# Expert weights in pairs of buffers, eight neighbouring rows per partition, in a diffusion backbone layer with expert-choice experts

## The chip, the cores and the metric

The kernel runs on one NeuronCore of a Trainium2 chip. The metric is the time of one execution on the device in microseconds (us). TensorE is called PE (PEld for its weight loads), VectorE DVE, ScalarE ACT, GpSimd POOL and SyncE SP. PEq, ACTq and SPq are the instruction queues of these engines.

## The reference

One layer works on 512 latent tokens of 1,024 features (and on 256 context tokens, which only feed the recurrence). First comes a token mixer: RMSNorm with adaLN shift and scale, one input projection, a Fourier branch and a recurrent branch, a gated merge, an output projection, a gated residual. Then the part that this change touches:

```
h  = rmsnorm(x) * (1 + sc2) + sh2                 # 512 x 1024
scores = softmax(h @ w_router)                    # 16 experts
g, idx = top 64 tokens of each expert by score
xg  = h[idx]                                      # 64 x 1024 for each expert
hid = silu(xg @ w_gate[e]) * (xg @ w_up[e])       # w_gate, w_up: 1024 x 1536
out = (hid @ w_down[e]) * g                       # w_down: 1536 x 1024
x  += g2 * scatter_add(out, idx)
y   = rmsnorm(x) * final_g
```

All of it is float32. The three weight matrices of 16 experts are 302 MB, read once from HBM.

## The kernel before

The first 405 us or so are the token mixer. Its weights come through staging tiles in pieces 256 columns (1 KB) wide. After it, w_out is applied in four column quarters, each token tile is squared and turned for the router, the softmax over the 16 experts is taken, and tokens are ranked by score.

Expert weights come in **units** of 128 x 1,536 floats, 6 KB on each partition (786,432 bytes). An expert has 24: eight of w_gate, eight of w_up, eight of w_down. Unit q of w_gate holds rows 128q to 128q+127, one row per partition, so partition p of unit k meets feature 128k+p. Units of w_down put six neighbouring rows on a partition and cut that run of 24 KB in four. The list `units` has them in the order in which PE reads them. The last expert's w_down is cut into nine pieces by output columns, with final_g ahead of them.

`eload()` issues the load of the next unit on SP's queue. Buffers go round: `NR = (14, 5, 1)` says how many lie in each of three rings (which open one after the other as the memory of the mixer and of the router comes free), two more are `held` in the staging tiles `wd` and `we`, and units 14 and 15 use two tiles lent by the staging area. So 22 units can be in SBUF. Each ring buffer is loaded again when PE has read it. 24 loads are issued ahead of the first expert; after that each unit read by `up_gate` (L1161) or by w_down's loop (L1260) is followed by one `eload()`. SP works through its loads strictly in order, and a load waits there for its buffer and for its turn among the semaphores that count DMAs. 

For two experts at a time, tokens are gathered by matmul: `gather_k` (L1133) multiplies a 128 x 128 block of x (the stationary operand, features 128k to 128k+127 of 128 tokens) with a one-hot matrix `oh` of the chosen tokens, over four token tiles. Each float32 matmul of this kind is two instructions. `gather_out_k` (L1139, L1141) applies shift (`modc`) and scale (`s2`), which lie feature 128k+p on partition p, column k, and writes `xg`. The gather of a pair comes at the end of the odd expert before it; experts 0 and 1 are gathered piece by piece (`one_k`, tile `xa`) within the first experts.

Within an expert: gate units, with the scatter of the previous expert between them (L1180); silu on ACT (L1222); up units, with the ranking of the expert after next; the gather in odd experts; six transposes of the hidden values, `sl[:, j:FH:6]`, every sixth element (L1248); w_down's units; the scaled output. At expert 2 ACT's queue copies half of `g2` into the spare end of `we` (L1240).

The end of the kernel adds the last expert's output in three column parts, normalises and stores four tiles `o` that reuse ring buffers (L1275 to L1305).

The shift's contribution to the router is made at L992 (matmuls `pb`) and L993 (copy to `bias`); behind it `ada_red` (L293, L300) reduces the last adaLN part, and L995 scales the router's weights. L430 is the matmul of w_out, L949 transposes x for the router.

Of the kernel before, what the change touches and what calls it, by code (L numbers as in the profile page):

```python
# [21 lines left out]
NT = T // P  # L22
# [12 lines left out]
def tables():  # L35
    quarter = D // 4
    f32 = np.float32
    freqs = np.exp(f32(-np.log(10000.0)) * np.arange(quarter, dtype=f32) / f32(quarter)).astype(f32)
    emb = np.zeros((64, 2, 512), f32)
    for i, n in ((0, T // GRID_W), (1, GRID_W)):  # L40
        ang = np.arange(n, dtype=f32)[:, None] * freqs
        emb[:n, i] = np.concatenate([np.sin(ang), np.cos(ang)], axis=-1)
    d = np.arange(P)
    a = 2 * np.pi * ((d[:, None] * d) % P) / P
    t = np.arange(258)
    dft_c = np.zeros((P, 387), f32)
    dft_c[:, 0:65] = np.cos(a[:, 0:65])
    dft_c[:, 65:129] = np.sin(a[:, 0:64])
    dft_c[0, 129:386] = np.where(np.arange(257) % 2, -1.0, 1.0) / 256.0
    dft_t = np.zeros((P, 2, 2, 258), f32)  # L50
    for b in range(2):
        m = ((P * b + d[:, None]) * t) % T
        dft_t[:, 0, b] = np.where(t < 257, np.cos(2 * np.pi * m / T) / 256.0, 0.0)
        dft_t[:, 1, b] = np.where((t < 256) & (m % 256 != 0), -np.sin(2 * np.pi * m / T) / 256.0, 0.0)
    p = np.arange(P)
    cst = np.zeros((P, 211), f32)
    cst[:, 0:128] = np.eye(P)
    for v in range(2):
        cst[:, 128 + v] = (p % 32 == v)
    for e in range(NE):  # L60
        cst[:, 130 + e] = (p % 32 == e)
    cst[:, 146:210] = np.arange(64)
    cst[:, 210] = p % 64
    tri = (p[:, None] < p[None, :]).astype(f32)
    sel = np.zeros((8, NT, P), f32)
    for n in range(NT):
        sel[:, n] = np.arange(8)[:, None] == 2 * n + p // 64
    rs = np.concatenate([emb[:8, 0], sel.reshape(8, -1)], axis=1)
    return {"rs": rs, "ce": np.concatenate([emb[:, 1]] * 2), "dft_c": dft_c, "dft_t": dft_t, "cst": cst, "tri": tri}


V_N2, V_CW, V_CB, V_LAM, V_BA, V_BI = 8, 16, 48, 56, 72, 88
# [4 lines left out]
def layer(ctx: ExitStack, tc: tile.TileContext, I, out):  # L77
    nc = tc.nc
    pe, act, dve, pool = nc.tensor, nc.scalar, nc.vector, nc.gpsimd
# [10 lines left out]
    def flat(ap, off, dims):  # L90
        return bass.AP(tensor=ap.tensor, offset=ap.offset + off, ap=[list(d) for d in dims])
# [6 lines left out]
    stage, close_stage = sb("stage")  # L98
# [9 lines left out]
    def gt(name):  # L108
        return ps.tile([P, 2, 512], F32, tag="g", bufs=2, name=name)
# [4 lines left out]
    x = keep.tile([P, NT, D], F32, name="x")  # L114
# [9 lines left out]
    s2 = keep.tile([P, KD], F32, name="s2")  # L124
# [739 lines left out]
    close_gp()  # L864
    close_hl()

    NR = (14, 5, 1)
    rings = [None] * 3
    edge, close_edge = open_pool("edge", side="right")
    edge.tile([P, 120], F32, name="edge")  # L870
# [10 lines left out]
    def eload():  # L881
        n = ring["n"]
        if n >= len(units):
            return
        ring["n"] += 1
        e, wn, q = units[n]
        if 0 <= n - NR[0] < 2:
            t = stage.tile([P, 2048], F32, tag="raw", bufs=AHEAD, name=f"lent{n}")[:, 0:DE]
        else:
            m, i = (n if n < NR[0] else n - 2) % (sum(NR) + 2), 0  # L890
            while i < 3 and m >= NR[i]:
                m, i = m - NR[i], i + 1
            t = rings[i].tile([P, DE], F32, tag="ew", bufs=NR[i], name=f"ew{n}") if i < 3 else held[m]
        if e == NE:
            t = t[:, 0:D]
            nc.sync.dma_start(t, flat(I["final_g"], 0, [[0, P], [1, D]]))
            EW["fg"] = t
            return
        src = I[wn][0, e]
        if wn == "w_down_e":  # L900
            if e == NE - 1:
                c0, cw, k0, nk = q
                f, j = divmod(k0, 6)
                t = t[:, 0:cw * nk].rearrange("p (k d) -> p k d", k=nk)
                nc.sync.dma_start(t, src[FH * f:FH * f + FH, c0:c0 + cw].rearrange("(p k) d -> p k d", k=6)[:, j:j + nk])
            else:
                f, j = divmod(q, 4)
                nc.sync.dma_start(t, src[FH * f:FH * f + FH, :].rearrange("(p k) d -> p (k d)", k=6)[:, DE * j:DE * j + DE])
        else:
            nc.sync.dma_start(t, src[P * q:P * q + P, :])  # L910
        EW[e, wn, q] = t


    rt, close_rt = sb("rt", "right")
    bias = rt.tile([P, NE], F32, name="bias")
    lg = rt.tile([P, NT, NE], F32, name="lg")
    mx = rt.tile([P, 2, NT], F32, name="mx")
    xT = rt.tile([P, KD, P], F32, name="xT")
# [79 lines left out]
    wa = stage.tile([P, 4, 512], F32, tag="raw", bufs=AHEAD, name="wa")  # L998
    sB, oh, trit = wa[:, 0, :], wa[:, 1, :].rearrange("p (n c) -> p n c", n=NT), wa[:, 2, 0:P]
    nc.sync.dma_start(trit, I["tri"])  # L1000
    eload()
    eload()
    dve.memset(oh, 0.0)

# [61 lines left out]
    eload()  # L1066
    g20 = we[:, DE:2048]
    sl = wc[:, 1280:2048]
# [61 lines left out]

    def gather_k(a, k, q):
        for n in range(NT):
            pe.matmul(a[k // 4][:, P * (k % 4) + q.start:P * (k % 4) + q.stop], x[:, n, P * k:P * k + P],  # L1133
                      oh[:, n, q], start=n == 0, stop=n == NT - 1)

    def gather_out_k(a, k, q):
        src = a[k // 4][:, P * (k % 4) + q.start:P * (k % 4) + q.stop]
        if k % 2 or k < 3 and q == h0:
            act.activation(xg[:, k, q], src, AF.Identity, bias=modc[:, 24 + k, 0:1], scale=s2[:, k:k + 1])  # L1139
        else:  # L1140
            dve.tensor_scalar(xg[:, k, q], src, s2[:, k:k + 1], modc[:, 24 + k, 0:1], op0=OP.mult, op1=OP.add)  # L1141

    def gather():
        a = [at("xg0"), at("xg1")]
# [8 lines left out]
    def up_gate(e, wn, name, hooks):  # L1153
        t = mps.tile([P, 2, 512], F32, tag=name, bufs=1, name=name)
        c = CAP * (e % 2)
        for k in range(KD):
            w = EW.pop((e, wn, k))
            for n in range(2):
                for f in range(2):
                    o = FH * f + 384 * n  # L1160
                    pe.matmul(t[64 * f:64 * f + 64, n, 0:384], xg[:, k, c:c + CAP], w[:, o:o + 384],  # L1161
                              start=k == 0, stop=k == KD - 1, tile_position=(0, 64 * f))
            if (e, wn) != (0, "w_up_e") or k < KD - 2:
                eload()
            for f in hooks.get(k, ()):
                f()
        return t
# [42 lines left out]
    for e in range(NE):  # L1210
# [44 lines left out]
        for q in range(KD):  # L1255
            w = EW.pop((e, "w_down_e", q))
            f = q // 4
            for i in range(3):
                j, dh = divmod(3 * (q % 4) + i, 2)
                pe.matmul(yp[64 * dh:64 * dh + 64, :], hT[j // 3][:, j % 3, 64 * f:64 * f + 64], w[:, 512 * i:512 * i + 512],  # L1260
                          start=f == 0 and j == 0, stop=f == 1 and j == 5, tile_position=(0, 64 * dh))
            eload()
# [9 lines left out]
    ov = out[0].rearrange("(n p) d -> p n d", p=P)  # L1272
    act.activation(ssb[:, 7:8], eps_t, AF.Sqrt)
    e = NE - 1
    os = [rings[0].tile([P, D], F32, tag="ew", bufs=NR[0], name=f"o{n}") for n in range(NT)]  # L1275
    sst = (ss[:, 0:NT], ssb[:, 0:NT], ss[:, 4:4 + NT])

    def out_a(p, n, mid=None):
# [111 lines left out]
```

## Time and profile before

| | us |
|---|---|
| median of three runs | 1171.66 |
| lowest, highest | 1169.88, 1172.23 |
| the profiled execution | 1173.57 |
| its span, first to last instruction | 1171.7 |

| engine | busy us | share of the span |
|---|---|---|
| PE | 1134.9 | 97% |
| PEld | 678.5 | 58% |
| DVE | 548.8 | 47% |
| ACT | 293.4 | 25% |
| POOL | 115.3 | 10% |

The profiled execution is one run of its own, a little longer than its span, since the launch and the end lie around the span. Busy shares are averages over the mixer and the experts, which have different limits. Matmuls overlap in PE's pipeline, so a PE that is busy all the time is not a PE at its peak. TensorE's granted clock is 0.996 of its full 2.4 GHz over the span. HBM reads are 364.43 MB, 313 GB/s over the span.

### The profile page before, as it was taken

Reading aid. Unit: us, or ns where it says so; the run is one execution under the profiler, and the core shown is the slowest. Engines: PE = TensorE matmul, PEld = TensorE weight load, DVE = VectorE, ACT = ScalarE, POOL = GpSimd, SP = SyncE. Lnnn points to the kernel's source line nnn. Section 1 sums busy time; section 2 is a strip of 40 time slices with the busy share of each in tenths; the row PEclk is TensorE's granted clock in tenths of the full one; section 3 lists DMA queues with packets and bytes.
Section 4 is the critical chain, followed back from the end, with each engine's and each line's share of the span. In section 5 each row is a group of like instructions: output and inputs, shape, how many; then the busy total and the mean of one; then the engine's idle time right before and its main releaser. Section 6 shows DMA issues by size and latency. Waiting matters only on the chain. (4 is left out here: it accounts for less than half of the span.)

```text
span 1171.7 us, 16760 instructions
## 1 busy us (share of the span) xinstructions
PE 1134.9 (97%) x6888; PEld 678.5 (58%) x6888; DVE 548.8 (47%) x1090; ACT 293.4 (25%) x457; POOL 115.3 (10%) x120
## 2 busy tenths in 40 slices
PE   8999999999999999999999999999999999999986
PEld 4778777777888996545445445454454344444333
DVE  4455989877776854332333342342332332332124
ACT  5462776665322132101001001001001001001004
POOL 5173343421000000000000000000000000000002
PEclk9999999999999999999999999999999999999998
DMA  8924322233546597899999999999999999999995
GB/s 309 298 74 128 126 81 72 100 108 108 180 158 202 187 415 295 308 369 420 369 425 423 424 424 424 424 423 424 424 423 424 424 424 423 423 425 423 424 414 214
DMA packets 115435, 368.01 MB, mean 314 GB/s; under 512 B 8912, under 2 KB 61656, under 8 KB 115232
## 3 DMA queue, kind: packets, MB, share of 16 engines
q1 hardware_dynamic: 112688, 363.52, 78.4%
q0 software_dynamic: 1088, 2.18, 0.6%
q10 hardware_dynamic: 1584, 1.25, 0.4%
q8 instruction: 54, 0.88, 0.3%
q14 instruction: 21, 0.17, 0.0%
HBM read 364.43 MB, written 2.10 MB: 313 GB/s over the span
## 5 line engine op out<-in xcount | busy, mean ns | idle before, releaser
L1161 PE MATMUL G<-ew,g 128*64 128x384 f32 x960 | 171.5, 493 | 2.5 <-DMA ew<-in_w_gate_e 2.0
L1161 PE MATMUL U<-ew,g 128*64 128x384 f32 x928 | 166.3, 493 | 6.8 <-DMA ew<-in_w_up_e 6.7
L1186 DVE TENSOR_TENSOR ac<-ac,sc 128x512 f32<-128x512 f32 x112 | 71.9, 684 | 97.5 <-PE sc L1180 97.5
L1161 PEld LDWEIGHTS G<-ew,g 128*64 128x64 f32 x960 | 63.0, 136 | 85.1 <-issue 64.3
L1161 PEld LDWEIGHTS U<-ew,g 128*64 128x64 f32 x928 | 60.6, 136 | 87.3 <-issue 59.5
L1297 POOL TENSOR_TENSOR o<-ac,ew 128x512 f32<-128x512 f32 (+1 forms) x8 | 7.8, 1001 | 873.7 <-ACT o L1293 873.7
L1263 DVE SCALAR_TENSOR_TENSOR wc<-Y,gc,g 128x512 f32<-128x512 f32 x15 | 11.3, 750 | 145.7 <-PE Y L1260 145.7
L1260 PE MATMUL Y<-ew,wa 128*64 128x512 f32 x312 | 74.1, 597 | 2.2 <-ACT wa L1249 2.2
L1260 PE MATMUL Y<-ew,wd 128*64 128x512 f32 x312 | 74.6, 594 | 0.0
L1249 ACT COPY wa<-T 128x384 f32<-128x384 f32 x16 | 7.7, 479 | 250.6 <-PE T L1248 250.6
L231 DVE TENSOR_TENSOR wL<-raw,wH 128x1024 fp32r<-128x1024 f32 x48 | 63.0, 1345 | 12.9 <-ACT wH L230 12.9
L1222 ACT ACTIVATE wc<-G 128x768 f32<-128x768 f32 x16 | 13.0, 811 | 180.9 <-PE G L1161 180.9
L230 ACT CAST wH<-raw 128x1024 fp32r<-128x1024 f32 x48 | 48.3, 1046 | 26.9 <-PE zO L430 18.5
L1133 PEld LDWEIGHTS xg<-wa,x 128*128 128x128 f32 x448 | 51.1, 192 | 0.2
L1133 PE MATMUL xg<-wa,x 128*128 128x128 f32 x448 | 51.2, 275 | 0.0
L1260 PEld LDWEIGHTS Y<-ew,wd 128*64 128x64 f32 x312 | 23.1, 137 | 47.3 <-issue 39.9
L1099 DVE TENSOR_SCALAR wc<-wa,score 128x128 bf16<-128x128 f32 (+3 forms) x63 | 23.9, 379 | 56.4 <-ACT wa L1092 56.4
L1266 ACT CAST wb<-wc 128x512 fp32r<-128x512 f32 x15 | 9.3, 618 | 153.2 <-DVE wc L1263 153.2
L1260 PEld LDWEIGHTS Y<-ew,wa 128*64 128x64 f32 x312 | 21.4, 136 | 43.8 <-issue 35.7
L1180 PEld LDWEIGHTS sc<-wb 64*128 64x128 f32 x240 | 23.6, 184 | 35.9 <-issue 35.9
L712 POOL TENSOR_TENSOR th<-tp,th 128x768 f32<-128x768 f32 x16 | 37.6, 2368 | 63.1 <-DVE tp L711 63.1
L688 ACT ACTIVATE th<-ga,lru_c 128x768 f32<-128x768 f32 x32 | 28.9, 905 | 41.8 <-PE ga L686 41.8
(361 smaller groups left out, 2167.2 us busy)
## 6 DMA issues: line engine op xcount, KB each, us to landing
ew<-in_w_gate_e SPq DMA_DIRECT2D x120, 768.0 KB, 14.7
ew<-in_w_up_e SPq DMA_DIRECT2D x116, 768.0 KB, 14.7
ew<-in_w_down_e SPq DMA_DIRECT2D x111, 768.0 KB, 14.7
raw<-in_w_ada SPq DMA_DIRECT2D x24, 1024.0 KB, 5.4
raw<-in_w_in SPq DMA_DIRECT2D x16, 1024.0 KB, 4.9
wd<-in_w_down_e SPq DMA_DIRECT2D x8, 768.0 KB, 11.9
we<-in_w_down_e SPq DMA_DIRECT2D x8, 768.0 KB, 14.7
raw<-in_w_lru SPq DMA_DIRECT2D x4, 1024.0 KB
```

What stands on the lines that cost most here:

```text
L230: (copy or act.copy)(wH[:, a], raw[:, a])
L231: dve.tensor_sub(wL[:, a], raw[:, a], wH[:, a].bitcast(F32))
L688: act.activation(t, gf[:, 256:1024], AF.Tanh, bias=(hbi if i else hba)[:, 8 * d + h:8 * d + h + 1], scale=0.5)
L712: pool.tensor_tensor(b, s, b, op=OP.mult)
L1099: dve.tensor_scalar(GT[c][:, 0:m], sB[:, 0:m], s, None, op0=OP.is_lt)
L1133: pe.matmul(a[k // 4][:, P * (k % 4) + q.start:P * (k % 4) + q.stop], x[:, n, P * k:P * k + P], oh[:, n, q], start=n == 0, stop=n == NT - 1)
L1161: pe.matmul(t[64 * f:64 * f + 64, n, 0:384], xg[:, k, c:c + CAP], w[:, o:o + 384], start=k == 0, stop=k == KD - 1, tile_position=(0, 64 * f))
L1180: pe.matmul(a[dh][:, c], w, v, start=j == 0, stop=j == 1, tile_position=(64 * dh, 0))
L1186: dve.tensor_add(xs, xs if e else x[:, n, q], a[dh])
L1222: act.activation(v3(sl), G[:, :, 0:384], AF.Silu)
L1260: pe.matmul(yp[64 * dh:64 * dh + 64, :], hT[j // 3][:, j % 3, 64 * f:64 * f + 64], w[:, 512 * i:512 * i + 512], start=f == 0 and j == 0, s ...
L1263: dve.scalar_tensor_tensor(y, yp, gc[:, e % 3:e % 3 + 1], g2, op0=OP.mult, op1=OP.mult)
```

## The change

Loads are issued two units at a time. A ring buffer becomes 12 KB wide (`NR = (7, 2, 1)` counts such pairs), `eload()` is called after every second unit, and one DMA fills both halves where both are whole units. The lent pair, the held pair and the pieces of the last expert keep one DMA for each.

w_gate and w_up are laid out like w_down: partition p holds the eight neighbouring rows 8p to 8p+7, and unit k is row 8p+k. Units k and k+1 are then one contiguous run of 12 KB on each partition. w_down's units j and j+1 were neighbours already.

The gather follows that order: block k of xg must hold features 8p+k, so the stationary operand is `x[:, n, k:D:KD]`, every eighth element. Shift and scale are brought into the same order once, by a matmul with a constant permutation `pm` (a new input, 128 x 144) and masks, into `vp`. The output tiles `o` become two tiles of two halves.

```diff
-    NR = (14, 5, 1)
+    NR = (7, 2, 1)
...
-        ring["n"] += 1
-        e, wn, q = units[n]
-        if 0 <= n - NR[0] < 2:
-            t = stage.tile([P, 2048], F32, tag="raw", bufs=AHEAD, name=f"lent{n}")[:, 0:DE]
+        ring["n"] += 2
+        m = n // 2
+        if m == NR[0]:
+            ts = [stage.tile([P, 2048], F32, tag="raw", bufs=AHEAD, name=f"lent{i}")[:, 0:DE] for i in range(2)]
         else:
...
+            if i < 3:
+                both = rings[i].tile([P, 2 * DE], F32, tag="ew", bufs=NR[i], name=f"ew{n}")
+                ts = [both[:, 0:DE], both[:, DE:2 * DE]]
+            else:
+                both, ts = None, held
+        e, wn, q = units[n]
+        if n // 2 != NR[0] and both is not None and e < NE and isinstance(q, int):
+            nc.sync.dma_start(both, e_rows(e, wn, q, 2))
+        else:
+            for t, u in zip(ts, units[n:n + 2]):
+                e_one(t, *u)
...
+    def e_rows(e, wn, q, m):
         src = I[wn][0, e]
         if wn == "w_down_e":
+            f, j = divmod(q, 4)
+            return src[FH * f:FH * f + FH, :].rearrange("(p k) d -> p (k d)", k=6)[:, DE * j:DE * (j + m)]
+        return src.rearrange("(p k) e -> p (k e)", k=KD)[:, DE * q:DE * (q + m)]
...
-            nc.sync.dma_start(t, src[P * q:P * q + P, :])
...
+    pm = rt.tile([P, 144], F32, name="pm")
+    nc.scalar.dma_start(pm, I["pm"])
...
     dve.tensor_copy(bias, g[:, 0, 0:NE])
+    for v, a in enumerate((s2, modc[:, 24:32, 0])):
+        dve.tensor_tensor(pv[:, v], a.unsqueeze(1).to_broadcast([P, KD, KD]),
+                          pm[:, 128:136].unsqueeze(2).to_broadcast([P, KD, KD]), op=OP.mult)
+    gv = gt("pv")[:, 0, 0:128]
+    pe.matmul(gv, pm[:, 0:128], pv.rearrange("p v a b -> p (v a b)"), start=True, stop=True)
+    for v in range(2):
+        dve.tensor_tensor(pv[:, v], gv[:, 64 * v:64 * v + 64].rearrange("p (a b) -> p a b", a=KD),
+                          pm[:, 136:144].unsqueeze(1).to_broadcast([P, KD, KD]), op=OP.mult)
+        dve.tensor_reduce(vp[:, v, :], pv[:, v], axis=AX.X, op=OP.add)
     ada_red()
...
-            pe.matmul(a[k // 4][:, P * (k % 4) + q.start:P * (k % 4) + q.stop], x[:, n, P * k:P * k + P],
+            pe.matmul(a[k // 4][:, P * (k % 4) + q.start:P * (k % 4) + q.stop], x[:, n, k:D:KD],
...
-            act.activation(xg[:, k, q], src, AF.Identity, bias=modc[:, 24 + k, 0:1], scale=s2[:, k:k + 1])
+            act.activation(xg[:, k, q], src, AF.Identity, bias=vp[:, 1, k:k + 1], scale=vp[:, 0, k:k + 1])
...
-            if (e, wn) != (0, "w_up_e") or k < KD - 2:
+            if k % 2 and ((e, wn) != (0, "w_up_e") or k < KD - 1):
                 eload()
...
-            eload()
+            if q % 2:
+                eload()
...
-    os = [rings[0].tile([P, D], F32, tag="ew", bufs=NR[0], name=f"o{n}") for n in range(NT)]
+    os = [t[:, i, :] for n in range(2) for t in [rings[0].tile([P, 2, D], F32, tag="ew", bufs=NR[0], name=f"o{n}")]
+          for i in range(2)]
```

## Rows read from the trace of the kernel before

**Rows 1.** Windows: us, busy us (instructions) by engine, PEclk, DMA share, GB/s.

```profile
568.00:572.00 4.00, 4.00 (x30) 1.85 (x28) 3.08 (x9) 0.28 (x1) 0.00 (x0) 1.00 0.52 172
572.00:576.00 4.00, 4.00 (x28) 1.72 (x24) 1.31 (x5) 0.00 (x0) 0.00 (x0) 1.00 0.76 276
...
580.00:1120.00 540.00, 528.63 (x3410) 246.40 (x3411) 167.98 (x387) 45.44 (x86) 0.00 (x0) 1.00 1.02 423
...
1140.00:1160.00 20.00, 18.51 (x107) 9.49 (x104) 7.45 (x13) 6.49 (x17) 5.55 (x5) 1.00 0.72 257
```

**Rows 2.** Timeline of PE where experts 3, 7, 9, 15 start: start, us, what.

```profile
591.05 2.75 PE L1161 MATMUL G<-ew,g 128*64 128x384 f32 x16
...
757.99 2.75 PE L1161 MATMUL G<-ew,g 128*64 128x384 f32 x16
...
841.54 1.51 PE L1161 MATMUL G<-ew,g 128*64 128x384 f32 x8
843.40 0.87 PE L1161 MATMUL G<-ew,g 128*64 128x384 f32 x4 [0.35 <-DMA ew<-in_w_gate_e]
...
1110.87 1.51 PE L1161 MATMUL G<-ew,g 128*64 128x384 f32 x8
```

**Rows 3.** DMA packets, queues and issues (the last: count, size, us to landing).

```profile
DMA packets 115435, 368.01 MB, mean 314 GB/s; under 512 B 8912, under 2 KB 61656, under 8 KB 115232
...
q8 instruction: 54, 0.88, 0.3%
...
ew<-in_w_gate_e SPq DMA_DIRECT2D x120, 768.0 KB, 14.7
...
out<-o SPq DMA_DIRECT2D x4, 512.0 KB, 2.6
```

**Rows 4.** Windows again, a stretch of the mixer with 1 KB runs.

```profile
360.00:380.00 20.00, 20.00 (x91) 16.30 (x90) 12.26 (x25) 5.57 (x8) 0.00 (x0) 1.00 0.61 204
```

**Rows 5.** Waits of SP's queue, 500 to 620 us: total us, times, longest.

```profile
SPq L910 <- DMA ew<-in_w_gate_e: 17.7, 12, 2.6
...
SPq L910 <- DMA we<-g: 11.5, 1, 11.5
```

**Rows 6.** Timeline of ACT's queue from 565 to 573 us.

```profile
567.70 1.15 ACTq L1240 DMA_DIRECT2D we<-g  x2
```

**Rows 7.** Single lines: durations in ns, least/median/most; first and last start.

```profile
L1133 PE MATMUL xg<-wa,x x448: 272/275/275, 534.2 to 1058.1; 128*128 128x128 f32 x150
...
L1248 PEld LDWEIGHTS T<-cst,wc x96: 209/236/242, 495.9 to 1142.6; 128*128 128x128 f32 x96
L1248 PE MATMUL T<-cst,wc x96: 293/297/402, 496.0 to 1142.7; 128*128 128x128 f32 x96
...
L949 PEld LDWEIGHTS xt<-cst,x x32: 137/140/224, 422.1 to 446.6; 128*128 128x128 f32 x32
L949 PE MATMUL xt<-cst,x x32: 271/272/307, 422.2 to 446.7; 128*128 128x128 f32 x32
```

**Rows 8.** Timeline of PE: a gather and two groups of transposes.

```profile
422.18 0.82 PE L949 MATMUL xt<-cst,x 128*128 128x128 f32 x6
...
701.13 7.31 PE L1133 MATMUL xg<-wa,x 128*128 128x128 f32 x64
708.28 0.96 PE L1248 MATMUL T<-cst,wc 128*128 128x128 f32 x6
```

**Rows 9.** Timelines of ACT, PE and DVE around the router's bias.

```profile
402.35 2.00 ACT L230 CAST wH<-raw 128x1024 fp32r<-128x1024 f32 x2 [8.57 <-PE zO L430]
...
414.11 1.96 PE L992 MATMUL pb<-wr,modc 128*128 128x16 f32 x16
415.92 0.68 PE L293 MATMUL adb<-acc,one_eps 128*128 128x256 f32 x2
...
416.11 0.17 DVE L993 COPY bias<-pb 128x16 f32<-128x16 f32 x1
...
417.08 0.29 DVE L995 TENSOR_TENSOR wr<-wr,s 128x128 f32<-128x128 f32 x1
```

More of the change, by code (lines that the diff above doesn't have):

```diff
@@ L64, in tables @@
     tri = (p[:, None] < p[None, :]).astype(f32)
+    k8 = np.arange(8)
+    pm = np.concatenate([p[:, None] // 8 == p[None, :] % 16, p[:, None] % 8 == k8, p[:, None] // 16 == k8], axis=1).astype(f32)
     sel = np.zeros((8, NT, P), f32)
@@ L68, in tables @@
     rs = np.concatenate([emb[:8, 0], sel.reshape(8, -1)], axis=1)
-    return {"rs": rs, "ce": np.concatenate([emb[:, 1]] * 2), "dft_c": dft_c, "dft_t": dft_t, "cst": cst, "tri": tri}
+    return {"rs": rs, "ce": np.concatenate([emb[:, 1]] * 2), "dft_c": dft_c, "dft_t": dft_t, "cst": cst, "tri": tri, "pm": pm}
 V_N2, V_CW, V_CB, V_LAM, V_BA, V_BI = 8, 16, 48, 56, 72, 88
@@ L884, in eload @@
             return
-        ring["n"] += 1
-        e, wn, q = units[n]
-        if 0 <= n - NR[0] < 2:
-            t = stage.tile([P, 2048], F32, tag="raw", bufs=AHEAD, name=f"lent{n}")[:, 0:DE]
-        else:
-            m, i = (n if n < NR[0] else n - 2) % (sum(NR) + 2), 0
+        ring["n"] += 2
+        m = n // 2
+        if m == NR[0]:
+            ts = [stage.tile([P, 2048], F32, tag="raw", bufs=AHEAD, name=f"lent{i}")[:, 0:DE] for i in range(2)]
+        else:
+            m = (m if m < NR[0] else m - 1) % (sum(NR) + 1)
+            i = 0
@@ L891, in eload @@
             while i < 3 and m >= NR[i]:
                 m, i = m - NR[i], i + 1
[L893 to L898, printed above, removed]
+            if i < 3:
[3 more added lines that the diff above has]
+                both, ts = None, held
@@ L899, in eload @@
+        e, wn, q = units[n]
[4 more added lines that the diff above has]
+                e_one(t, *u)
+        for t, u in zip(ts, units[n:n + 2]):
+            if u[0] < NE:
+                EW.setdefault(u, t)
+    def e_rows(e, wn, q, m):
         src = I[wn][0, e]
         if wn == "w_down_e":
[L901 to L908, printed above, removed]
-        else:
-            nc.sync.dma_start(t, src[P * q:P * q + P, :])
@@ L911, in eload, with e_one @@
-        EW[e, wn, q] = t
+            f, j = divmod(q, 4)
+            return src[FH * f:FH * f + FH, :].rearrange("(p k) d -> p (k d)", k=6)[:, DE * j:DE * (j + m)]
+        return src.rearrange("(p k) e -> p (k e)", k=KD)[:, DE * q:DE * (q + m)]
+    def e_one(t, e, wn, q):
+        if e == NE:
+            EW["fg"] = t[:, 0:D]
+            nc.sync.dma_start(EW["fg"], flat(I["final_g"], 0, [[0, P], [1, D]]))
+        elif isinstance(q, int):
+            nc.sync.dma_start(t, e_rows(e, wn, q, 1))
+        else:
+            c0, cw, k0, nk = q
+            f, j = divmod(k0, 6)
+            t = EW[e, wn, q] = t[:, 0:cw * nk].rearrange("p (k d) -> p k d", k=nk)
+            nc.sync.dma_start(t, I[wn][0, e][FH * f:FH * f + FH, c0:c0 + cw].rearrange("(p k) d -> p k d", k=6)[:, j:j + nk])
@@ L914, in layer @@
     rt, close_rt = sb("rt", "right")
     bias = rt.tile([P, NE], F32, name="bias")
+    pm = rt.tile([P, 144], F32, name="pm")
+    nc.scalar.dma_start(pm, I["pm"])
+    pv = rt.tile([P, 2, KD, KD], F32, name="pv")
+    vp = lru_c[:, 0, :].rearrange("p (v k) -> p v k", v=2)
     lg = rt.tile([P, NT, NE], F32, name="lg")
@@ L1065, in layer @@
     eload()
-    eload()
     g20 = we[:, DE:2048]
@@ L1138, in gather_out_k @@
         if k % 2 or k < 3 and q == h0:
-            act.activation(xg[:, k, q], src, AF.Identity, bias=modc[:, 24 + k, 0:1], scale=s2[:, k:k + 1])
+            act.activation(xg[:, k, q], src, AF.Identity, bias=vp[:, 1, k:k + 1], scale=vp[:, 0, k:k + 1])
         else:
-            dve.tensor_scalar(xg[:, k, q], src, s2[:, k:k + 1], modc[:, 24 + k, 0:1], op0=OP.mult, op1=OP.add)
+            dve.tensor_scalar(xg[:, k, q], src, vp[:, 0, k:k + 1], vp[:, 1, k:k + 1], op0=OP.mult, op1=OP.add)
     def gather():
@@ L1261, in layer @@
                           start=f == 0 and j == 0, stop=f == 1 and j == 5, tile_position=(0, 64 * dh))
-            eload()
+            if q % 2:
+                eload()
         dve.scalar_tensor_tensor(y, yp, gc[:, e % 3:e % 3 + 1], g2, op0=OP.mult, op1=OP.mult)
```

## The prediction, made before the changed kernel was run

> **What bounds the kernel now.** Read the busy table by stretch first [rows 1]. From 580 to 1120 us, 46% of the span, the sixteen DMA engines are at a share of 1.02 and deliver 423 GB/s without a break. PE looks as busy (528.6 of 540 us), so that column cannot say which of the two sets the pace. The timeline of PE by experts can [rows 2]: expert 3 starts at 591.05, expert 7 at 757.99, that is 83.47 us for a pair of experts (an odd one and an even one). Two experts bring 48 buffers of 786,432 bytes, 37.75 MB; at 423 GB/s they take 89.2 us. DMA is the slower of the two. PE does not feel it at first, because it begins with 22 buffers filled ahead and eats that lead. From expert 9 on it does: the start at 841.54 is followed by the next unit 1.86 us later, with a wait for the DMA, where sixteen matmuls (two units, 1.29 us apart) took 2.75 us before. From 841.54 to the start of expert 15 at 1110.87 are 269.3 us; three free-running pairs would take 250.4. So PE has 18.9 us of slack by then, and some more inside expert 15.
>
> The end is therefore the last byte plus a fixed tail (after 1140 the share drops to 0.72 and PE finishes alone [rows 1]). The last byte moves in two ways: by the rate, and by every stretch in which the DMA engines had nothing to do before they became the bound. The last such hole is at 568 to 576 us (shares 0.52 and 0.76), worth, in us, 4 x (1 - 172/423) + 4 x (1 - 276/423) = 3.8 us. Before it, buffers are full and loads wait for PE to free one, so a delay of PE there delays the loads one for one. After it, PE delays are free until the slack is gone. That split prices every part below.
>
> **Part 1, runs of 12 KB instead of 6 KB.** A packet is one contiguous run: 115,232 of 115,435 packets are under 8 KB, and the instruction queue moved 0.88 MB in 54 packets, 16 KB each, so a 12 KB packet can exist [rows 3]. What a packet costs beside its bytes is seen by comparing two stretches. Where 1 KB runs load, a share of 0.61 gives 204 GB/s [rows 4]: 334 GB/s per full share, 49.0 ns a packet. In [rows 1] 423 GB/s at 1.02 is 414.7 per full share, 237.0 ns per 6 KB packet. The slope is (237.0 - 49.0)/5,120 bytes, 37.6 ns per KB, so 11.4 ns are fixed. The share above 1 says packets overlap: one 6 KB packet starts every 232.4 ns, so 4.6 of the 237.0 are already hidden and 6.8 show. Two such packets take 464.8 ns, one of 12 KB 458.0: the rate rises 1.5%, to 429 GB/s. Bounds: nothing (if a run is cut in two again), and 2.5% (all 11.4 ns saved). Not every load gets it. Of 376 whole units, the pair lent from the staging buffers and the 17 pairs that fall on the two separate held buffers stay single; 340 units, 90%, become 170 long loads. 1.5% x 0.90 over 559 us (580 to about 1139, when the last whole unit is in; the pieces of the last expert are cut as before) is **-7.4 us**; bounds 0 and -12.5.
>
> The Trainium skill, "DMA: Bandwidth & Descriptors", section Bandwidth, has a fixed cost of about 3 cycles of a 32-byte bus per packet; by that, 390 cycles become 387, 0.8%, and the term would be an estimated -4 us. The rows show a larger fixed part.
>
> **Part 2, gather with stride.** With eight neighbouring rows of a weight matrix on a partition, xg must hold features 8p+k, so the stationary operand of the gather becomes every eighth element of x, 32 bytes apart. The gather's matmuls are 64 per pair of experts in 7.31 us [rows 8], (7.31 - 0.28)/63 = 111.6 ns apart (0.28 being one matmul's duration [rows 7]), with weight loads back to back: nothing hides a longer load. The trace has no 32-byte stride, but it has one of 24 bytes: the six transposes of L1248 read every sixth element. They stand (0.96 - 0.30)/5 = 132 ns apart; the six of L949, same shape and contiguous, (0.82 - 0.27)/5 = 110 ns. That is +22 ns for a strided load. The load's own duration rises more, from 140 to 236 ns [rows 7], +96, but most of that overlaps. Bounds: 0 and 96; I take 22, since spacing is what the gather pays. There are 88 such loads for experts 0 and 1 and 64 in expert 1's gather, all before the hole: 152 x 22 ns = **+3.3 us** on the path (0 to 14.6). The six later gathers add 384 x 22 ns = 8.4 us of PE, which the slack covers.
>
> The Trainium skill, "SBUF — State Buffer", section Door 1, gives a reason: lines of 16 bytes, and each access that crosses to a new one pays, so four fp32 are as far as one strides for free. By that rule 24 and 32 bytes pay alike and the sum below stays; the trace agrees that 24 pays, and no row shows 32.
>
> **Part 3, shift and scale in the new order.** pm is one more load on ACT's queue, needed at about 416 us. What queues behind it are ACT's casts of w_out, before which ACT idles 8.57 us for PE [rows 9]: 0, or some tenths if its memory comes free late. Two DVE products, a matmul, two more products and two reductions stand between the bias copy and the reduction of adaLN. PE is in order, so its next matmul, now at 415.92, waits: the bias copy ends at 416.28 [rows 9], two products of 64 columns at 0.17 to 0.29 us each follow, then the new matmul's two passes, some 0.2. The adaLN matmul starts near 416.9: **+1.0 us** (0.5 to 2). Behind it on DVE the products and reductions delay the split of w_out's last columns by about a microsecond more; PE has the 24 matmuls of the first tile of w_out's third quarter before it needs them. This slip reaches expert 0 whole.
>
> **Part 4, buffers in pairs.** The ring still has 20 buffers and two held ones. While it is full, a load now starts when the second unit of its pair is read rather than the first: up to one unit late, which is 2.75/2 = 1.4 us [rows 2], or 0.7 more where a scatter stands between. Once DMA is the bound it costs nothing, since buffers are then free long before. **+1.4 us** (0 to 2.1). The pair in the router's old memory is one buffer more than before that waits for it; the DMA queue has others to move, and PE reads it as its twenty-first unit: 0. The output tiles are pairs too. If the second half had to wait for the first half's store, that would be up to one store, 2.6 us [rows 3]; I take 0, since the halves are stored by DMAs of their own.
>
> **Part 5, the hole.** Loads land 14.7 us after issue [rows 3], 7.9 times the 1.86 us of one, so eight are in flight: each waits for the one eight before, as the queue's waits show [rows 5]. One waited 11.5 us for something else, the small copy of g2 into `we`, which has a turn among the eight. That copy was issued at 567.70 [rows 6], and while the loads stood behind it the DMA engines ran dry: this is the hole. With pairs, eight turns cover 16 units; the load that meets the copy's turn comes some six units later in the stream, when PE has yet to free its buffer anyway. The hole should close: **-3.8 us** (0 to -3.8).
>
> **Sum.** -7.4 - 3.8 + 3.3 + 1.0 + 1.4 = -5.5 us. PE allows it: 1.0 + 3.3 + 8.4 = 12.7 of its 18.9 us of slack. The profiled execution took 1173.57 us (span 1171.7), 1.9 above the median of the three runs; it would become 1168.1, and the median 1166.2.
>
> **Rivals.** (A) *The strided load costs much more than 22 ns.* Every load counts once PE is the bound: 536 x extra + 1.0 against 18.9 us of slack, or an estimated 24 if half of expert 15's sixteen steps are late by 1.86 - 1.29 us too. It turns slower at 33 to 43 ns; at 60 ns it is 33.2 - 18.9 = +14 (+9 with the larger slack), at the duration's 96 ns +28 to +34. For it: the 236 ns of [rows 7], and 32 is a wider step than 24. Against: matmuls follow the spacing, not the duration. 1180 to 1205; chance 0.20. (B) *DMA is no faster*: the run is cut, or what limits 423 GB/s is not the packet. Then -3.8 + 5.7 = +1.9, or +5.7 if the hole also stays: 1173 to 1178. For it: no 12 KB load was measured; against: at a share of 1.02 the DMA engines themselves are full, and a packet has a fixed part. 0.12. (C) *The strided load is free*, or all 11.4 ns are saved: -9 to -14, 1158 to 1163. For it: the later transposes may owe their spacing to the moving side. 0.13. The forecast itself: 0.55, with 1161 to 1169 as its own range.
>
> **Range and chances.** Leaving out the far part of A and the bottom of C gives 1158 to 1180. The runs of before spread over 0.2%, so 0.2% (2.3 us) is about what can be told from no change. Faster: nearly all of the forecast and C, 0.66; within: part of B and a sliver of the forecast, 0.10; slower: A and the rest of B, 0.24.
>
> **What will show it.** Rate: 429 GB/s in the stretch from 580 on, and about 93,700 packets in all. Stride: 64 gather matmuls in 8.7 us rather than 7.31 (8.7 = 0.28 + 63 x 134 ns); over 10 us means rival A. Order: the adaLN matmul starts 1 us later behind the bias copy. Hole: shares of 1.0 from 520 us on. PE: the last experts still show unit steps that wait for DMA, but fewer; none at all with a later end means A. The forecast is wrong if the rate stays at 423, or if pairs of experts exceed 88 us with no DMA wait.

## The result, and the profile after

The changed kernel takes 1220.53 us (median of four runs, 1215.04 to 1224.50) beside 1171.95 for the kernel before on the same chip: 1.0386 times as long, 95% interval 1.035 to 1.0423 (the two medians by themselves stand as 1.0415). 1166.2 was forecast, with a range up to 1180. This is rival A, and further out than rival A was drawn.

First the page of the kernel after: the DMA packets, and the gather's group of instructions (busy us, mean ns of one, idle before).

```profile
DMA packets 91096, 368.05 MB, mean 302 GB/s; under 512 B 6208, under 2 KB 59080, under 8 KB 69136
...
L1161 PE MATMUL xg<-wa,x 128*128 128x128 f32 x448 | 107.5, 401 | 0.0
```

The packets answer to [rows 3]: the 12 KB packets are there, since fewer than before are below 8 KB and the bytes are the same. The forecast had about 93,700 packets in all; the 2,600 that are gone beyond that are small ones (6,208 under 512 B rather than 8,912), some 16 for each of the 170 DMAs saved. The matmul of the gather now takes 401 ns where [rows 7] has 275. The windows say who sets the pace (columns as in [rows 1]: busy us of PE, PEld, DVE, ACT and POOL, granted clock, DMA share, GB/s).

```profile
580.00:1120.00 540.00, 537.37 (x3284) 287.77 (x3294) 168.04 (x395) 44.01 (x83) 0.00 (x0) 1.00 0.99 415
1140.00:1160.00 20.00, 18.71 (x112) 8.00 (x109) 2.24 (x3) 1.69 (x3) 0.00 (x0) 1.00 1.01 428
```

From 580 to 1120 us the DMA engines move 415 GB/s at a share of 0.99, where they had 423 at 1.02. They are not slower: in the second of these windows they reach 428. They run out of free buffers, because PE is late: in the 540 us of the first window SP's queue waits 171.5 us for PE to read buffers of w_down (tile Y), 122.9 for w_gate (G) and 109.9 for w_up (U).

```profile
SPq L903 <- PE Y L1288: 171.5, 40, 19.7
```

PE's timeline shows by how much it is late, first the starts of experts 0, 3, 7, 9 and 15, with the gather in expert 5.

```profile
465.67 2.83 PE L1189 MATMUL G<-ew,g 128*64 128x384 f32 x8
...
617.50 2.75 PE L1189 MATMUL G<-ew,g 128*64 128x384 f32 x16
...
735.63 15.36 PE L1161 MATMUL xg<-wa,x 128*128 128x128 f32 x64
...
800.54 2.75 PE L1189 MATMUL G<-ew,g 128*64 128x384 f32 x16
...
892.05 2.75 PE L1189 MATMUL G<-ew,g 128*64 128x384 f32 x16
...
1165.18 2.75 PE L1189 MATMUL G<-ew,g 128*64 128x384 f32 x16
```

The 64 matmuls take 15.36 us where [rows 8] has 7.31: (15.36 - 0.40)/63 = 237 ns apart rather than 111.6, **+126 ns for each strided load**. Experts 3 to 7 take 183.04 us rather than 166.94 [rows 2]: two pairs, 16.1 us more, two gathers of 64 loads at 126 ns. A pair is now 91.5 us, longer than the 89.2 us in which DMA brought its weights. Expert 9 starts with sixteen matmuls in one run, without the wait for a DMA that [rows 2] shows at 843.40, and so does expert 15. By the forecast's own sign ("none at all with a later end means A") the bound has moved to PE.

**Where the 47 us are.** The profiled executions differ by 1220.66 - 1173.57 = 47.1 us, the spans by 47.2. Expert 0 starts 6.6 us later (459.02 before), expert 3 26.4 later [rows 2], expert 15 54.3 later, and from there to the end 7.1 us are won back. Per step: seven pair gathers cost 8.0 us each, 56.2 in all; the 72 loads in expert 0 cost 9.1 and the 16 ahead of it 2.0; the new work for shift and scale 1.0. That is 68.3. Against it stand the waits for DMA that are gone. From expert 3 to expert 15 it was 519.82 us and is 547.68, 27.9 more, where six of the gathers bring 48.2: the kernel before had waited 20.3 us there. The last expert gives the 7.1. 68.3 - 27.4 = 40.9. The other 6.3 us lie before expert 1: 2.1 had been lost by the time the router's bias starts (416.21 against 414.11 [rows 9]), where PE has issued the same instructions in both kernels (the granted clock was 0.83 from 40 to 60 us, where the kernel before had 1.00); the rest, 1.5 and 2.7, goes with two stretches at the lower clock, the window from 420 to 424 us (0.68) and the one shown at the end.

The step that the forecast priced at +1.0 us, on PE's timeline:

```profile
416.21 1.96 PE L1013 MATMUL pb<-wr,modc 128*128 128x16 f32 x16
418.70 0.49 PE L1019 MATMUL pv<-pv,pm 128*128 128x128 f32 x2 [0.54 <-DVE pv L1016]
419.03 0.94 PE L295 MATMUL adb<-acc,one_eps 128*128 128x256 f32 x2
```

From the first bias matmul to the adaLN matmul it is 2.82 us, and was 1.81 [rows 9].

### The profile page after: what moved, and what is told of

Its sections match the earlier page's. It is cut to its first block, busy times and chain, and to the rows that moved or that the text cites. A ratio compares the mean times of both kernels' runs of the same rounds, so it can differ in the third digit from the quotient of the medians.

```text
span 1218.9 us, 16399 instructions
## 1 busy us (share of the span) xinstructions
PE 1191.8 (98%) x6872; PEld 754.4 (62%) x6890; DVE 550.0 (45%) x1096; ACT 293.3 (24%) x457; POOL 115.4 (9%) x120
## 2 busy tenths in 40 slices
DMA packets 91096, 368.05 MB, mean 302 GB/s; under 512 B 6208, under 2 KB 59080, under 8 KB 69136
## 4 chain that ended last, share of the span: by engine, by line
PE 87%; DVE 4%; ACT 4%; POOL 1%; DMA 1%; issue 1%; SPq 0%; ACTq 0%; POOLq 0%; DVEq 0%
PE G L1189 14%; PE U L1189 14%; PE Y L1288 13%; PE xg L1161 9%; PE zB L432 4%; PE yR L432 4%; PE sc L1208 3%; PE zX L764 3%; PE zA L432 3%; PE zO L432 3%; PE ga L687 2%; PE xa L1161 2%; PE zF L432 2%; PE zX L765 2%; PE ga L688 1%
## 5 line engine op out<-in xcount | busy, mean ns | idle before, releaser
L1189 PE MATMUL U<-ew,g 128*64 128x384 f32 x928 | 161.6, 491 | 0.0
L1161 PEld LDWEIGHTS xg<-wa,x 128*128 128x128 f32 x448 | 107.7, 336 | 0.0
L1161 PE MATMUL xg<-wa,x 128*128 128x128 f32 x448 | 107.5, 401 | 0.0
L1288 PE MATMUL Y<-ew,wd 128*64 128x512 f32 x312 | 71.4, 592 | 0.0
L1169 DVE TENSOR_SCALAR g<-xg,lru_c 128x128 f32<-128x128 f32 x28 | 10.8, 407 | 108.6 <-ACT g L1167 66.3
```

## The experiments

**1. A ladder of steps.** Theory: a strided stationary operand of a float32 matmul has a price of its own, and the transposes were the wrong row to take it from. Rivals: the price grows evenly with the step, or 32 bytes are special. Behind the last store of the kernel before, twenty equal matmuls for each step:

```diff
+    xf = x.rearrange("p n d -> p (n d)")
+    for s, nm in ((1, "la"), (2, "lb"), (3, "lc"), (4, "ld"), (5, "le"), (6, "lf"), (7, "lg"), (8, "lh"), (12, "li"), (16, "lj")):
+        a = at(nm)
+        for i in range(20):
+            pe.matmul(a[:, 0:P], xf[:, 0:P * s:s], oh[:, 0, :], start=True, stop=True)
+    for s, nm in ((1, "ta"), (4, "td"), (6, "tf"), (8, "th")):
...
+            pe.transpose(a[:, 0:P], xf[:, 0:P * s:s], ident)
+    for s, nm in ((1, "wa"), (8, "wh")):
...
+            pe.matmul(a, xf[:, 0:P * s:s], xf[:, 0:512], start=True, stop=True)
```

> The kernel before, with weight loads of x at steps of 1, 2, 3, 4, 5, 6, 7, 8, 12 and 16 floats measured by themselves behind the last store (20 float32 matmuls each, 128 moving columns, plus transposes at steps 1, 4, 6, 8, plus 512 moving columns at steps 1 and 8). Its own time says nothing. Theory 1 (a 32-byte step is dear in itself): step 1 near 112 ns from matmul to matmul, step 8 near 237 as in the changed kernel. If the price goes by 16-byte lines, steps 1 and 2 cost the same and 4 to 16 all cost the same; if it goes by the bytes spanned, it grows evenly (18 ns at step 2, 54 at 4, 90 at 6, 126 at 8, 270 at 16); if 32 bytes meet one bank over and over, 8 and 16 stand out and 5, 6, 7 stay near the 22 ns that the transposes at step 6 showed. Theory 2 (the gather is slow for another reason, such as what it runs beside): step 8 stays below 140 ns here.

PE's timeline; the name of the output tells the step, and the start of the next row less the start of this one, over the count, is the spacing (five of the rows behind the table are left out). Each of the twenty float32 matmuls is two instructions here, x40 in the row, and each transpose is one; prices are for one instruction. The granted clock is 1.00 throughout.

```profile
1175.93 4.62 PE L1357 MATMUL la<-wa,x 128*128 128x128 f32 x40
1180.39 4.88 PE L1357 MATMUL lb<-wa,x 128*128 128x128 f32 x40
1185.10 7.10 PE L1357 MATMUL lc<-wa,x 128*128 128x128 f32 x40
1192.04 9.49 PE L1357 MATMUL ld<-wa,x 128*128 128x128 f32 x40
...
1228.60 9.70 PE L1357 MATMUL lh<-wa,x 128*128 128x128 f32 x40
...
1257.54 2.35 PE L1361 MATMUL ta<-cst,x 128*128 128x128 f32 x20
1259.72 2.58 PE L1361 MATMUL td<-cst,x 128*128 128x128 f32 x20
1262.14 2.89 PE L1361 MATMUL tf<-cst,x 128*128 128x128 f32 x20
1264.87 2.40 PE L1361 MATMUL th<-cst,x 128*128 128x128 f32 x20
1267.11 17.33 PE L1365 MATMUL wax<-x 128*128 128x512 f32 x40
1284.28 17.33 PE L1365 MATMUL whx<-x 128*128 128x512 f32 x40
```

| step in floats | 1 | 2 | 3 | 4 | 5 | 6 | 7 | 8 | 12 | 16 |
|---|---|---|---|---|---|---|---|---|---|---|
| matmul, ns | 111.5 | 117.8 | 173.5 | 233.3 | 223.3 | 224.0 | 233.5 | 238.3 | 266.8 | 218.5 |
| transpose, ns | 109.0 | | | 121.0 | | 136.5 | | 112.0 | | |

Step 8 costs a matmul +127 ns, what the gather lost. It is not even in the step, and 32 bytes are not special: a matmul pays 6 ns at 2 floats, 62 at 3 and 122 at 4, and from there on between 107 and 155. The transposes, from which the forecast took its price, pay 27 at the same step of 6 at which a matmul pays 112, and 2 to 3 at a step of 8. With 512 moving columns the two steps stand the same, 429 ns apart: there the load is hidden.

The Trainium skill, "SBUF — State Buffer", section Door 1, says two things in one note: two hits in a 16-byte line are needed for full bandwidth, and four fp32 are as far as one strides for free. The ladder agrees with the first (two floats, two hits: +6) and not with the second (four floats: +122).

**2. The change without the stride.** The kernel after with the gather's operand contiguous again. The features of xg are then out of order against the weights; loads and work are those of the change.

```diff
-            pe.matmul(a[k // 4][:, P * (k % 4) + q.start:P * (k % 4) + q.stop], x[:, n, k:D:KD],
+            pe.matmul(a[k // 4][:, P * (k % 4) + q.start:P * (k % 4) + q.stop], x[:, n, P * k:P * k + P],
```

> The changed kernel with the gather's stationary operand contiguous again; shift, scale and weights stay in the new order, so the features that the experts see are out of order and only the time counts. Theory 1: the gather takes 7.3 us again for 64 matmuls and the rest of the forecast holds, 8 to 9 us faster than before, ratio 0.992, with 429 GB/s and unit steps that wait for DMA in the late experts. Theory 2 (pairs or long runs cost something themselves): between 1172 and 1200 us, ratio over 1.0.

1169.20 us, ratio 0.9951 (0.9925 to 0.9978). The gather takes 7.31 us again. Its windows:

```profile
500.00:520.00 20.00, 19.73 (x120) 8.27 (x119) 6.34 (x14) 1.48 (x3) 0.00 (x0) 1.00 0.89 360
...
540.00:560.00 20.00, 19.79 (x129) 12.29 (x130) 3.99 (x9) 2.50 (x6) 0.00 (x0) 1.00 0.99 404
560.00:580.00 20.00, 20.00 (x138) 9.27 (x136) 9.47 (x22) 2.02 (x3) 0.00 (x0) 1.00 1.01 423
580.00:1120.00 540.00, 524.24 (x3456) 250.95 (x3466) 171.16 (x394) 45.39 (x86) 0.00 (x0) 1.00 1.01 428
```

428 GB/s where the forecast had 429, and the hole at 568 to 576 us is closed. But DMA now rests at 500 to 520 and at 540 to 560, where SP waits for PE to read w_down's units: 14.2 us from 500 to 520, where the kernel before waited 5.8. Against 428 the windows from 500 to 600 lose 5.3 us; those of the kernel before (387, 424, 417, 345, 423) lose 5.7 against 423. What the closed hole gave, the loads in pairs took back almost whole.

**3. The stride without the change.** The kernel before with only the gather's operand strided; the features are again out of order.

```diff
-            pe.matmul(a[k // 4][:, P * (k % 4) + q.start:P * (k % 4) + q.stop], x[:, n, P * k:P * k + P],
+            pe.matmul(a[k // 4][:, P * (k % 4) + q.start:P * (k % 4) + q.stop], x[:, n, k:D:KD],
```

> The kernel before with the strided gather alone; weights keep their order, so the features are out of order and only the time counts. Theory 1: 536 loads at 126 ns more are 67 us of PE, less some 24 us of slack: 1172 + 43 = 1215 us, ratio 1.037, PE never waiting for DMA in the late experts. Theory 2: under 1185 us.

1215.03 us, ratio 1.0349 (1.0318 to 1.0380). One line gives nearly the whole loss: 41.2 us between the medians, where the change lost 48.6. Its long window is that of the kernel after:

```profile
580.00:1120.00 540.00, 537.39 (x3272) 287.43 (x3284) 166.18 (x391) 43.85 (x83) 0.00 (x0) 1.00 1.00 414
```

**4. Two rows per partition.** If two floats are nearly free, 12 KB runs can be had without the price: partition p holds rows 2p and 2p+1 of a block of 256 rows, so that a run of two rows is 12 KB and the gather steps by 8 bytes. Shift and scale are ordered to match.

```diff
-        return src.rearrange("(p k) e -> p (k e)", k=KD)[:, DE * q:DE * (q + m)]
+        return src[2 * P * (q // 2):2 * P * (q // 2) + 2 * P].rearrange("(p k) e -> p (k e)", k=2)[:, DE * (q % 2):DE * (q % 2 + m)]
...
-            pe.matmul(a[k // 4][:, P * (k % 4) + q.start:P * (k % 4) + q.stop], x[:, n, k:D:KD],
+            pe.matmul(a[k // 4][:, P * (k % 4) + q.start:P * (k % 4) + q.stop], x[:, n, 2 * P * (k // 2) + k % 2:2 * P * (k // 2) + 2 * P:2],
```

> The changed kernel with the permutation confined to blocks of 256 rows: partition p holds rows 256b+2p and 256b+2p+1, so a pair of units is still one run of 12 KB, and the gather's step is 2 floats, 8 bytes. If the price of a step goes by 16-byte lines, 8 bytes are free: like the contiguous run, ratio 0.992, 1163 us. If it goes by the bytes spanned, 18 ns a load: 2.7 us before DMA is the bound, the rest in PE's slack, ratio 0.995. Theory 2: over 1.0.

1170.04 us, ratio 0.9965 (0.9947 to 0.9983): some 50 us faster than the kernel after, and a little faster than the kernel before (the interval lies below 1). The long window is at 428 GB/s again, and the gather:

```profile
706.99 7.69 PE L1163 MATMUL xg<-wa,x 128*128 128x128 f32 x64
```

7.69 us is 0.38 more than [rows 8], 6 ns a load, as the ladder has it.

**5. Which side, and how wide.** A second ladder: the strided operand on the moving side, an ordinary matmul with the identity, transposes again, and narrower and wider matmuls at steps 1 (`ca`) and 8 (`ch`).

```diff
+    for s, nm in ((1, "ma"), (4, "md"), (6, "mf"), (8, "mh")):
...
+            pe.matmul(a[:, 0:P], oh[:, 0, :], xf[:, 0:P * s:s], start=True, stop=True)
+    for s, nm in ((1, "ia"), (6, "if"), (8, "ih")):
...
+            pe.matmul(a[:, 0:P], xf[:, 0:P * s:s], ident, start=True, stop=True)
...
+    for c in (64, 192, 256, 384):
+        for s, nm in ((1, "ca"), (8, "ch")):
...
+                pe.matmul(a[:, 0:c], xf[:, 0:P * s:s], xf[:, 0:c], start=True, stop=True)
```

> Before with a second ladder behind its last store, so its own time says nothing. It asks why transposes were a bad proxy for the gather's matmuls, and how wide a matmul must be to hide a strided load. Theory 1 (a stationary operand pays for its step, a transpose is another kind of load): matmuls with a contiguous stationary operand and a moving operand at steps 1, 4, 6 and 8 floats all stand about 111 ns apart; an ordinary matmul with the identity as moving operand pays as in the first ladder (about 224 at step 6, 238 at step 8), while the transposes repeat 137 and 112. With more moving columns the pair of instructions is limited by the longer of the two, the load (238) or the columns (429/512 = 0.84 ns each): contiguous about 112, 161, 215, 322 ns at 64, 192, 256 and 384 columns, step 8 about 238, 238, 238, 322. Rival (the transposes hold their data on the moving side, and the moving side has a price of its own): moving steps 6 and 8 show +27 and +2 ns as the transposes do.

```profile
1174.30 4.62 PE L1357 MATMUL ma<-x,wa 128*128 128x128 f32 x40
1178.76 9.36 PE L1357 MATMUL md<-x,wa 128*128 128x128 f32 x40
...
1197.10 9.51 PE L1357 MATMUL mh<-x,wa 128*128 128x128 f32 x40
1206.43 4.65 PE L1361 MATMUL ia<-cst,x 128*128 128x128 f32 x40
...
1219.86 9.68 PE L1361 MATMUL ih<-cst,x 128*128 128x128 f32 x40
1229.38 2.35 PE L1365 MATMUL ta<-cst,x 128*128 128x128 f32 x20
...
1253.51 4.48 PE L1370 MATMUL ca<-x 128*128 128x256 f32 x20
1257.82 4.92 PE L1370 MATMUL ch<-x 128*128 128x256 f32 x20
1262.58 6.61 PE L1370 MATMUL ca<-x 128*128 128x384 f32 x20
1269.03 6.61 PE L1370 MATMUL ch<-x 128*128 128x384 f32 x20
```

Both expectations fail for the moving side: it pays as much as the stationary one, 111.5 ns at step 1, 229.5 at 4, 233 at 8. So a strided operand of a float32 matmul pays on either side. The identity as such is not what makes transposes cheap: multiplied in the ordinary way it costs 112 and 238. The widths came as theory 1 said: 215 against 238 ns at 256 columns, the same 322 or so at 384. (At 64 and 192 columns part of the matmuls ran at the lower clock, so those are not compared here.) A matmul of this kind hides the price from somewhere between 256 and 384 moving columns.

**6. Pairs without long runs.** The second experiment's kernel (order of features as there) with two DMAs of 6 KB runs for each pair of buffers.

```diff
-        if n // 2 != NR[0] and both is not None and e < NE and isinstance(q, int):
-            nc.sync.dma_start(both, e_rows(e, wn, q, 2))
-        else:
-            for t, u in zip(ts, units[n:n + 2]):
-                e_one(t, *u)
+        for t, u in zip(ts, units[n:n + 2]):
+            e_one(t, *u)
```

> The changed kernel with a contiguous gather (features then out of order, as in the second run) in which each pair of buffers is filled by two DMAs of 6 KB runs at the same place of the ring. Theory 1 (the packet's length sets the rate): 423 GB/s again in the stretch from 600 to 1100 us, packets of 234 ns, and about 7 us more than the second run: ratio 1.000 to 1.002. Rival (the rate comes from the pairing, fewer waits and issues on SP's queue): 428 to 429 GB/s and ratio 0.995 as in the second run.

1178.70 us beside 1176.67, ratio 1.0019 (0.9995 to 1.0042): theory 1, in that the pairs of buffers alone gain nothing. A long load has both longer runs and fewer DMAs, and no run takes these two apart, so which of them raises the rate stays open. Its long window:

```profile
580.00:1120.00 540.00, 528.95 (x3412) 247.13 (x3422) 168.30 (x392) 44.77 (x85) 0.00 (x0) 1.00 1.02 423
```

The hole of [rows 1] is back in this kernel. The copy of g2 is issued at 575.72 us, and behind it SP's queue waits as long as in [rows 5]:

```profile
576.00:580.00 4.00, 4.00 (x30) 1.88 (x28) 3.06 (x9) 0.30 (x1) 0.00 (x0) 1.00 0.56 138
```

```profile
SPq L920 <- DMA we<-g: 11.5, 1, 11.5
```

In the second experiment's kernel the copy is issued at 574.64, and the share of the same window is 1.02. The two kernels differ in the DMAs alone, so it is the long loads that close the hole.

**7. Shift and scale later.** The fourth kernel with the permutation behind the first tile of w_out's fourth quarter.

```diff
-    gv = gt("pv")[:, 0, 0:32]
-    pe.matmul(gv, pm[:, 0:128], pv.rearrange("p v a b -> p (v a b)"), start=True, stop=True)
...
         r_pose_a(n)
+        if n == 0:
+            gv = gt("pv")[:, 0, 0:32]
+            pe.matmul(gv, pm[:, 0:128], pv.rearrange("p v a b -> p (v a b)"), start=True, stop=True)
...
```

> The fourth run's kernel (two rows per partition, 12 KB runs, gather step of 8 bytes) with the products, the permutation matmul and the reductions for shift and scale moved behind the first tile of w_out's fourth quarter, so that PE does not wait for DVE between the bias and the adaLN matmul. Theory 1 (the wait of 1.0 us reaches expert 0 whole and expert 0's start reaches the end, since DMA buffers are full before it): the adaLN matmul starts about 1.0 us earlier relative to the bias matmuls, the ratio falls from 0.9965 to about 0.9957. Rival (the wait was covered: what PE then waits for is DVE or the casts of w_out behind it): expert 0 starts no earlier relative to the bias matmuls, ratio unchanged.

1168.89 us beside 1176.67, ratio 0.9918 (0.9880 to 0.9956). On the same chip the kernel of 6 KB pairs had 1178.70. The adaLN matmul is back at 1.81 us behind the first bias matmul (4th kernel: 2.64):

```profile
412.71 1.96 PE L1013 MATMUL pb<-wr,modc 128*128 128x16 f32 x16
414.52 0.68 PE L295 MATMUL adb<-acc,one_eps 128*128 128x256 f32 x2
```

But expert 0 starts no earlier: 46.3 us after that bias matmul (459.0 - 412.71), 45.9 in the fourth kernel. The waits of PE between the two show why:

```profile
PE lp L980 <- DVE xT L974: 0.7, 1, 0.7
```

The fourth kernel does not have this wait, nor one of 0.2 us for DVE's x (L954). The products now stand in DVE's queue ahead of what the router needs. The rival holds: the wait moved. The better ratio than the fourth run's is not shown to come from this edit: the intervals of the two ratios overlap, the two kernels' long windows are alike (427 and 428 GB/s), and TensorE's mean granted clock was 0.994 in these runs beside 0.992 in those of the kernel before on that chip (fourth run: 0.992 beside 0.993).

**8. Types, and small steps on the moving side.**

```diff
+    xb = x[:, 3, :].bitcast(BF16)
+    dve.memset(xb, 1.0)
+    for s, nm in ((1, "ba"), (2, "bb"), (4, "bd"), (8, "bh"), (16, "bp")):
+        a = at(nm)
+        for i in range(40):
+            pe.matmul(a[:, 0:P], xb[:, 0:P * s:s], xb[:, 0:P], start=True, stop=True)
...
+    for s, nm in ((1, "ma"), (2, "mb"), (3, "mc"), (4, "md")):
...
+            pe.matmul(a[:, 0:P], oh[:, 0, :], xf[:, 0:P * s:s], start=True, stop=True)
```

> Before with a third ladder behind its last store, so its own time says nothing. Theory 1 (what counts is how many bytes lie between elements, two to a 16-byte line being free): bfloat16 loads at steps 1, 2 and 4 elements (2, 4, 8 bytes) stand alike, steps 8 and 16 (16 and 32 bytes) cost some 120 ns more each; float32 loads repeat the first ladder (111, 118, 233, 238 ns at steps 1, 2, 4, 8); a float32 moving operand goes the same way: about 111, 118, 173 and 234 ns at steps 1, 2, 3 and 4. Rival (what counts is the step in elements): bfloat16 pays from step 4 on. Rival (a moving operand pays for any step): the float32 moving operand costs 230 ns at step 2 already.

```profile
1173.40 2.40 PE L1359 MATMUL bd<-x 128*128 128x128 bf16 x40
1175.64 2.64 PE L1359 MATMUL bh<-x 128*128 128x128 bf16 x40
1178.12 2.64 PE L1359 MATMUL bp<-x 128*128 128x128 bf16 x40
...
1213.15 4.70 PE L1367 MATMUL mb<-x,wa 128*128 128x128 f32 x40
1217.69 7.09 PE L1367 MATMUL mc<-x,wa 128*128 128x128 f32 x40
1224.61 9.37 PE L1367 MATMUL md<-x,wa 128*128 128x128 f32 x40
```

The moving side goes step by step like the stationary one: 111.5, 113.5, 173, some 230 ns (for the last, with no row behind it, the duration less one matmul over 39). For bfloat16 both expectations fail: 56 ns at 4 elements (8 bytes), 62 at 8 and 16 (16 and 32 bytes), so +6 where float32 pays +122. Bytes between elements alone don't set the price. How much of a bfloat16 load's price the 128 columns hide was not tried.

**9. Step 4 in the kernel itself.**

```diff
-            pe.matmul(a[k // 4][:, P * (k % 4) + q.start:P * (k % 4) + q.stop], x[:, n, P * k:P * k + P],
+            pe.matmul(a[k // 4][:, P * (k % 4) + q.start:P * (k % 4) + q.stop], x[:, n, 4 * P * (k // 4) + k % 4:4 * P * (k // 4) + 4 * P:4],
```

> Before with the gather's stationary operand at a step of 4 floats (features of a block of 512 taken four apart), loads and everything else as in before; the features of xg are out of order against the weights. Theory 1 (a cliff between 2 and 4 floats, as in the ladder: +6 at 2, +122 at 4): unit step with the gather 18.6 us instead of 10.81, pairs of experts 91.2 us, no unit waits for DMA, ratio 1.031 to 1.036. Rival (the price grows evenly from +6 at 2 floats to +126 at 8, +46 at 4): gather step 13.7 us, 536 loads make 25 us against 27 of slack, ratio 0.999 to 1.004.

1211.73 us, ratio 1.0329 (1.0294 to 1.0363), the gather at

```profile
732.75 14.99 PE L1133 MATMUL xg<-wa,x 128*128 128x128 f32 x64
```

That is (14.99 - 0.40)/63 = 232 ns a load, the cliff between 2 and 4 floats, in place. 536 loads x 122 ns less the 27.4 us of waits that vanish are 38.0 us; 1211.73 less 1171.85 is 39.9.

## Why the prediction was wrong

**Part 2 failed, and it decided the result: the price of a strided load.** The forecast put 22 ns on each, and the gather paid 126. "Spacing is what the gather pays" was right, but the spacing was read from transposes, and they are not that kind of instruction. The same step of 24 bytes costs a transpose 27 ns and a float32 matmul 112 (experiment 1). The gather's step costs 126, above even the 96 ns taken as the upper bound: the duration of a load in [rows 7], rejected as mostly overlapped, was nearer than the spacing, and it too was a transpose's. A bound from another kind of instruction bounded nothing. That transposes of the kernel step by 6 and not by 8 made it worse: at a step of 8 the proxy would have said +2 or 3.

**What followed from it was right.** Rival A's working (every load counts once PE is the bound, less the slack) with 126 in it and the measured slack gives 536 x 0.126 - 27.4 = +40 for the stride alone, and experiment 3 measures +41.2 (1215.03 - 1173.83). The slack of 18.9 to 24 us was too small: expert 14 runs 1.4 us shorter than a free expert was taken to be, and the last expert and the tail gave 7.1.

**Part 1 held in size.** The window has 428 GB/s, against 429 for the 90% of the units that come in long loads; over the 559 us that is 6.5 us beside the forecast's 7.4. The ratios of experiments 2 and 6 lie 0.7% or 8 us apart (6.7 by the medians), if ratios taken on two chips may be set side by side, but that holds part 5's hole too. Why the rate rises, by the packet as argued or by the DMA, was not separated.

**Part 3 held**: +1.0 us in its place. The move of experiment 7 did not win it back: the wait turned up behind DVE's queue.

**Part 5 held, part 4 was too small.** Forecast -3.8 and +1.4. The hole at 568 to 576 us closed in experiment 2 (the window from 560 to 580 loses 3.5 us less), and came back in experiment 6 with loads of 6 KB runs, two DMAs to a pair, as the argument of the eight turns has it. But loads in pairs start later: the other windows from 500 to 600 lose 3.1 us more than before, not 1.4. Together they came to -0.4 us instead of -2.4. This did not decide the sign. In the changed kernel itself the sign "shares of 1.0 from 520 us on" failed, with 0.60 from 560 to 580, the window behind the first long gather.

The rest of the forecast's sum (-5.5, less the 3.3 of the stride: -8.8) answers to the -5.8 us of experiment 2 (0.9951 of 1173.83; the medians differ by 4.6). Left open is why a transpose pays so little. The 6.3 us by which the profiled execution exceeds the steps are put down to the clock by their place and were not tried.

## What to carry to other kernels

Before a layout puts a step into a float32 matmul's operand, take the price from a matmul of the same type and width: here +6 ns at 2 floats, +122 at 4, and nothing to gain from a proxy that is a transpose or bfloat16. Long loads with runs of 12 KB are worth having (423 to 428 GB/s), but two neighbouring rows per partition give them as well as eight, at a step that costs almost nothing. And slack on the engine that is second is small when both are near full: a pair of experts took PE 83.5 us and DMA 89.2, which left 5.7 us for each pair, and one line used 8.

## What the runs showed of the hardware that was not expected

The price of a step falls alike on the moving and the stationary operand of a float32 matmul (233 and 238 ns at step 8), is hidden from somewhere between 256 and 384 moving columns, is 6 ns for bfloat16 at the same 32 bytes, and is 2 to 3 ns for a float32 transpose.

The granted clock falls to its lower level (1.2 GHz, 0.50 in the column) for some microseconds at different places in runs of the same instructions. In the kernel after it did so within the first gathers:

```profile
460.00:464.00 4.00, 3.52 (x29) 2.94 (x29) 3.58 (x14) 0.12 (x1) 0.00 (x0) 0.94 1.00 424
464.00:472.00 8.00, 8.00 (x48) 5.44 (x49) 2.06 (x9) 1.09 (x3) 0.00 (x0) 0.50 0.29 120
```

PE was busy throughout those 8 us, and for 3.52 of the 4 ahead of them. The kernel of experiment 6, whose gather is contiguous, shows the same at the same place:

```profile
464.00:472.00 8.00, 8.00 (x49) 4.41 (x46) 1.23 (x6) 0.40 (x1) 0.00 (x0) 0.51 0.18 73
```

so it isn't the stride that does it.

The lower clock costs a strided load next to nothing. Eight strided loads of 64 columns in the kernel after, first inside that stretch and then at full clock, and eight contiguous ones of experiment 6 inside its stretch:

```profile
468.43 2.16 PE L1161 MATMUL xa<-wa,x 128*128 128x64 f32 x8
...
496.36 2.12 PE L1161 MATMUL xa<-wa,x 128*128 128x64 f32 x8
...
465.97 1.97 PE L1158 MATMUL xa<-wa,x 128*128 128x64 f32 x8
```

The contiguous ones take 1.10 us at full clock (489.00 in the same trace) and nearly twice as long at half of it; the strided ones take the same at either. What a strided load waits for does not slow down with TensorE's clock in these rows; what it is, they don't show.
